# 512-column matmuls in the merge and in both FFNs' first projections of a two-block transformer kernel, with the halves added on two engines

## The chip, the cores and the metric

The kernel runs on one core of one Trainium2 chip. The metric is the device time of one execution in microseconds, as the median of several runs. The core has a matrix engine (PE), which writes only into PSUM, and three engines that matter here besides: DVE (vector), ACT (scalar) and SP, which issues the transfers. Each engine executes its own list of instructions in order and waits on semaphores for the others.

## The reference, cut to what matters

Two transformer blocks over 256 tokens of width 1024, all in 32-bit floats. The first block has an attention branch and a recurrent branch, which are merged under two gates and projected; then comes a gated FFN of hidden width 2816. The second block has other mixers and a convolutional FFN.

```python
ya = jnp.einsum('bse,ed->bsd', y_attn, w_branch_attn[layer])
yb = jnp.einsum('bse,ed->bsd', y_hgrn, w_branch_hgrn[layer])
merged = jax.nn.sigmoid(gate_a) * ya + jax.nn.sigmoid(gate_b) * yb
h = h + jnp.einsum('bsd,de->bse', merged, w_out[layer])
u = rmsnorm(h, norm_ffn_g[layer])
z = (jax.nn.silu(jnp.einsum('bsd,df->bsf', u, w_ffn_gate[layer]))
     * jnp.einsum('bsd,df->bsf', u, w_ffn_up[layer]))
h = h + jnp.einsum('bsf,fd->bsd', z, w_ffn_down[layer])
...
def conv_ffn(h, w_up, conv_w, w_down):
    u = causal_dwconv(h @ w_up, conv_w)
    g, val = jnp.split(u, 2, axis=-1)
    return (jax.nn.silu(g) * val) @ w_down
```

## The kernel before, in words

Activations lie transposed: 128 features on the partitions, 256 tokens along the row, and a 1024-wide activation is 8 such tiles (index `k`). A product in full precision is made of three products in a reduced format: each activation is kept as a high part and a low part, side by side in one tile ([high 256 | low 256]), and each weight tile is split on the chip into `wh` (high) and `wl` (low). `wload` does this for each weight block of 128 x 1024: SP fetches it into `raw` (5 buffers), ACT makes `wh = raw` rounded, and DVE makes `wl = raw - wh` (5 buffers each).

A `gemm` makes one output tile of 128 features x 256 tokens in PSUM, over 8 values of `k` (22 in the FFNs' down projections). For each `k`, `mm3` issues either three 256-column matmuls, which add into the same 256 columns (wh with high, wh with low, wl with high: below "narrow"), or, when it is given a PSUM bank of 512 columns, two matmuls ("wide"): wh with [high | low] into all 512 columns, and wl with high into the upper 256. A wide gemm leaves two halves in PSUM that have to be added to each other.

```python
if ps.n == 2 * S:
    calls = [(ps, a, both, first, last), (ps[:, 1, :], b, hi, False, False)]
    pr.group(calls[::-1] if last else calls)
else:
    pr.group([(ps, a, hi, first, False), (ps, a, lo, False, False), (ps, b, hi, False, last)])
```

Before the change only the down projections use the wide form (7 of their 8 gemms in each FFN); there both halves are added to the residual by two DVE instructions. All else is narrow.

In the order of the program: the first block's mixers (to about 182 us); the merge (gates `wi[T_GA+f]`, `wi[T_GB+f]`, branch projections `wba`, `wbh`, output projection `wo`, 8 gemms each); FFN 1 (`wg`, `wu`: 22 gemms each, of which the first 4 run on activations that aren't normalised yet, then `wd`); the second block's mixers; FFN 2 (`wup`: 44 gemms, the first 4 likewise early, two of them per hidden tile `f`, then 3-tap convolution on DVE, then `wd2`). Between FFN 1's gemms DVE also makes the conditioning vector of the second block: `ada`, 48 products of a fetched 128 x 1024 block (`raw<-in_wada`) with a row held on the chip.

The instruction lists are not written by hand: `record` states the operations, and a list scheduler (`schedule`) orders them on each engine by keys (the PE time at which they are recorded, with offsets for chains and a lead for weights), by modelled durations and by free buffers. An operation made by `either` may go to ACT or DVE: it goes to the second engine only if the first is late, and in the first part of the program only if its key lies `altp1` behind the current time. PSUM has 8 banks, and a bank is handed out per gemm or per two narrow gemms.

Of the kernel before, what the change touches and what calls it, by code (L numbers as in the profile page):

```python
# [10 lines left out]
F32 = mybir.dt.float32  # L11
# [33 lines left out]
for _n, _w in ROW:  # L45
# [7 lines left out]


OPT = dict(
    split=213.902, altp1=0.203, altw1=145.239, o_n3=-12.83, s_n3=0.086, o_f=-0.19, s_f=0.011, lead=9.18,
    tp=2.16, la=42.517, hold=3.107, ahead=1.8, law=0.52, altp=2.588, altw=971.26, ada=0, o_h=11.785, s_h=0.932,
    o_a1=-5.477, s_a1=0.401, o_s=-9.529, s_s=0.517, o_so=-12.055, s_so=0.458, o_a2=1.603, s_a2=0.292,
    o_r=-7.576, s_r=0.015, o_n1=7.29, s_n1=0.166, o_n2=-14.801, s_n2=0.119, o_n4=-10.886, s_n4=0.057,
# [444 lines left out]
def record(pr, d):  # L504
# [13 lines left out]
    def bank2():  # L518
        return bank([P, 2, S])
# [85 lines left out]
    def gemm(ps, src, hl, nk=KD):  # L605
        for k0 in range(0, nk, 8):
            n = min(8, nk - k0)
            w = wload(src[:, k0:k0 + n, :], n * P)
            for i in range(n):
                mm3(ps, w, i, hl, k0 + i, k0 + i == 0, k0 + i == nk - 1)  # L610

    def gemm_multi(ws, pss, hl, parts):
        order = [k for p in parts for k in p]
        for part in parts:
            for j in range(len(pss)):
                for k in part:
                    mm3(pss[j], ws[j], k, hl, k, k == order[0], k == order[-1])
# [414 lines left out]
    hA = hl_of(yA)  # L1032
    ma = Q_all.rearrange("p a b s -> p (a b) s")
    for f in range(8):
        b = bank2()
        gemm(b[:, 0, :], wi[T_GA + f], hl)
        ada(1, OPT["ada"])
        gemm(b[:, 1, :], d["wba"][f], hA)
        sg = pr.tile([P, S], F32, "un", "sga", 3)
        act(sg, b[:, 0, :], AF.Sigmoid, bias=V("b_in", T_GA + f))  # L1040
        tt(ma[:, f, :], b[:, 1, :], sg, ALU.mult)
    yH = pair("yh", "yh")
    for p in range(4):
        f2 = slice(2 * p, 2 * p + 2)
# [3 lines left out]
    mg = pair("ya", "mg")  # L1048
    hH, hM = hl_of(yH), hl_of(mg)
    for f in range(8):  # L1050
        b = bank2()
        gemm(b[:, 0, :], wi[T_GB + f], hl)
        ada(1, OPT["ada"])
        gemm(b[:, 1, :], d["wbh"][f], hH)
        m = pr.tile([P, S], F32, "un", "sgb", 3)
        act(m, b[:, 0, :], AF.Sigmoid, bias=V("b_in", T_GB + f))
        tt(m, b[:, 1, :], m, ALU.mult)
        tt(m, m, ma[:, f, :], ALU.add)
        split(mg[0][:, f, :], mg[1][:, f, :], m)

# [2 lines left out]
    gffn = lambda f: V("norm_ffn_g", f)  # L1063
    for f in range(KD):
        b = bank2()
        gemm(b[:, 0, :], d["wo"][f], hM)
        tt(h[:, f, :], b[:, 0, :], h[:, f, :], ALU.add)
        scaled(xg, h, gffn, f)
        st2.add(h[:, f, :])

# [18 lines left out]
    for p in range(NFF // 2):  # L1089
        if p == 0:  # L1090
            sg = sg0
            for j in range(2):
                tt(sg[:, j, :], sg[:, j, :], r, ALU.mult)
                tt(sg[:, j, :], gb[2 + j][:, 0, :], sg[:, j, :], ALU.mult)
        else:
            b = bank2()
            for j in range(2):
                gemm(b[:, j, :], d["wg"][2 * p + j], hl)
            ada(1, OPT["ada"])
            sg = t2([P, 2, S], "sg")  # L1100
            act(sg, b, AF.Silu)
            b2 = bank2()
            for j in range(2):
                gemm(b2[:, j, :], d["wu"][2 * p + j], hl)
            ada(1, OPT["ada"])
            tt(sg, b2, sg, ALU.mult)
        t, o = divmod(2 * p, 8)
        split(z[t][0][:, o:o + 2, :], z[t][1][:, o:o + 2, :], sg)
    tt(g1e, V("norm_final_g", 0, 8), V("norm_final_g", 0, 8), ALU.mult)
# [256 lines left out]
    for f in range(NFF):  # L1366
        t = t2([P, 2, S], "sg")
        if 2 * f < NG:
            src = [fb[2 * f], fb[2 * f + 1]]
        else:  # L1370
            b = bank2()
            gemm(b[:, 0, :], wup[f], hl)
            gemm(b[:, 1, :], wup[NFF + f], hl)
            src = [b[:, 0, :], b[:, 1, :]]
        for j in range(2):
            g = f + j * NFF
            either(t[:, j, :], src[j], V("fw2", g))
# [149 lines left out]
```

## Time and profile before

| | us |
|---|---|
| median of 3 runs | 767.82 (767.16 to 768.51) |
| the profiled execution, its own time | 766.82 |
| its span, first to last instruction | 765.0 |
| PE busy in the span | 754.7 (99%) |
| DVE busy | 606.1 (79%) |
| ACT busy | 501.6 (66%) |
| granted clock of the matrix engine, mean | 0.998 |

The profiled execution's time is 1.0 us below the median of the runs, and 1.8 us of it lie outside the span. PE's busy time is modelled from pipelined instructions: its length in one row is longer than the distance to the next one's start. So distances between starts tell PE's pace, not the lengths of its rows. The same holds in part on DVE and ACT, whose instructions overlap their successors by some 0.08 us.

### The profile page before, as it was taken

The numbers are of one execution on the slowest core, as the hardware profiler recorded it, in microseconds if no ns is written. First come the engines' busy times: TensorE is split into PE (matmuls) and PEld (weight loads), VectorE is DVE, ScalarE is ACT, GpSimd is POOL, SyncE is SP. The second block draws the span as 40 slices with busy tenths as digits, with TensorE's granted clock in tenths as the row PEclk, the third lists the DMA queues.
The fourth block names the chain that finished last, engine by engine and source line by source line (L and its number), as shares of the span: only waits on it lengthen the run. The fifth ranks groups of instructions, "written<-read, shape, count | busy, mean of one in ns | idle before, by whom it ended". The sixth has DMA issues, their size and how long they took to land.

```text
span 765.0 us, 15411 instructions
## 1 busy us (share of the span) xinstructions
PE 754.7 (99%) x6058; PEld 733.5 (96%) x6058; DVE 606.1 (79%) x1117; ACT 501.6 (66%) x915; POOL 2.2 (0%) x13
## 2 busy tenths in 40 slices
PE   8999999999999999999999999999999999999995
PEld 7999999999999999999998899999999999999885
DVE  6798797877687789877768988988699987887652
ACT  6679999987444666444444457859878766666541
POOL 1000000000000000000000000000000000000000
PEclk9999999999999999999999999999999999999999
DMA  8953444478887558988778985483454775666621
GB/s 296 305 185 117 166 140 138 140 252 287 295 273 242 181 177 279 317 284 280 279 256 260 320 287 193 141 274 114 138 196 136 208 223 180 189 179 179 185 92 55
DMA packets 47512, 161.34 MB, mean 211 GB/s; under 512 B 5568, under 2 KB 7760, under 8 KB 47312
## 3 DMA queue, kind: packets, MB, share of 16 engines
q1 hardware_dynamic: 47152, 160.10, 63.8%
q8 instruction: 47, 0.77, 0.4%
q10 hardware_dynamic: 288, 0.26, 0.1%
q14 instruction: 25, 0.20, 0.1%
HBM read 159.03 MB, written 1.06 MB: 209 GB/s over the span
## 4 chain that ended last, share of the span: by engine, by line
PE 98%; DMA 1%; DVE 0%; SPq 0%; ACT 0%; DVEq 0%; issue 0%
PE ps L307 91%; PE ps L320 3%; PE ps L297 2%; PE ps L327 2%; DMA raw<-in_wv_dram 1%; SPq L334 0%; DVE ot L269 0%; DVE wl L269 0%; ACT wh L229 0%; ACT r L229 0%; DVEq L1522 0%; DVE ot L275 0%; DVE x L275 0%; ACT sql L229 0%
## 5 line engine op out<-in xcount | busy, mean ns | idle before, releaser
L229 ACT ACTIVATE wh<-raw 128x1024 fp32r<-128x1024 f32 (+3 forms) x253 | 258.2, 1028 | 188.5 <-PE ps L307 114.5
L269 DVE TENSOR_TENSOR wl<-raw,wh 128x1024 fp32r<-128x1024 f32 (+3 forms) x255 | 299.0, 1182 | 75.5 <-ACT wh L229 74.4
L307 PE MATMUL ps<-uf,wh 128*128 128x256 f32 x1280 | 226.6, 280 | 0.0
L307 PEld LDWEIGHTS ps<-uf,wh 128*128 128x128 f32 x1280 | 196.9, 189 | 0.0
L307 PE MATMUL ps<-u,wh 128*128 128x256 f32 x976 | 183.2, 287 | 0.0
L307 PE MATMUL ps<-uf,wl 128*128 128x256 f32 x640 | 180.2, 282 | 0.0
L307 PEld LDWEIGHTS ps<-u,wh 128*128 128x128 f32 x976 | 149.4, 189 | 0.8 <-issue 0.4
L307 PE MATMUL ps<-u,wl 128*128 128x256 f32 x488 | 136.9, 281 | 0.0
L307 PE MATMUL ps<-z,wh 128*128 128x512 f32 (+1 forms) x396 | 122.5, 369 | 0.0
L307 PEld LDWEIGHTS ps<-uf,wl 128*128 128x128 f32 x640 | 120.5, 188 | 0.0
L307 PE MATMUL ps<-z,wl 128*128 128x256 f32 x352 | 96.4, 280 | 0.0
L307 PEld LDWEIGHTS ps<-u,wl 128*128 128x128 f32 x488 | 91.9, 188 | 0.0
L275 DVE SCALAR_TENSOR_TENSOR raw<-raw,crow 128x1024 f32<-128x1024 f32 x48 | 58.5, 1222 | 32.1 <-DMA raw<-in_wada_dram 31.2
L307 PEld LDWEIGHTS ps<-z,wh 128*128 128x128 f32 x396 | 70.5, 188 | 12.4
L307 PEld LDWEIGHTS ps<-z,wl 128*128 128x128 f32 x352 | 66.3, 188 | 1.1
L307 PE MATMUL ps<-xg,wh 128*128 128x256 f32 (+1 forms) x256 | 46.5, 284 | 0.0
L307 PEld LDWEIGHTS ps<-xg,wh 128*128 128x128 f32 x256 | 39.6, 189 | 0.2
L229 ACT ACTIVATE ax<-ax,ast 128x256 f32<-128x256 f32 (+1 forms) x82 | 35.2, 447 | 3.9 <-DVE ast L729 3.9
L307 PE MATMUL ps<-xg,wl 128*128 128x256 f32 (+1 forms) x128 | 36.0, 281 | 0.0
L275 DVE SCALAR_TENSOR_TENSOR sg<-ps,vec_t,sg 128x255 f32<-128x255 f32 (+1 forms) x80 | 32.9, 473 | 0.3 <-ACT sg L229 0.3
L307 PE MATMUL ps<-wh,xg 128*128 128x384 f32 x96 | 25.1, 341 | 0.7 <-ACT wh L229 0.7
L307 PEld LDWEIGHTS ps<-xg,wl 128*128 128x128 f32 x128 | 24.4, 190 | 0.0
(259 smaller groups left out, 1024.5 us busy)
## 6 DMA issues: line engine op xcount, KB each, us to landing
raw<-in_wi_dram SPq DMA_DIRECT2D x49, 512.0 KB, 4.6
raw<-in_wada_dram SPq DMA_DIRECT2D x48, 512.0 KB, 4.6
raw<-in_wup_dram SPq DMA_DIRECT2D x44, 512.0 KB, 3.6
raw<-in_wd_dram SPq DMA_DIRECT2D x32, 512.0 KB, 4.2
raw<-in_wg_dram SPq DMA_DIRECT2D x22, 512.0 KB, 4.4
raw<-in_wu_dram SPq DMA_DIRECT2D x22, 512.0 KB, 4.6
raw<-in_w_dram SPq DMA_DIRECT2D x20, 512.0 KB, 4.2
raw<-in_wo_dram SPq DMA_DIRECT2D x16, 512.0 KB, 4.1
```

Source lines behind the costliest of these rows:

```text
L229: self.nc.scalar.activation(out.real(), in_.real(), func, **kw)
L269: f = lambda: self.nc.vector.tensor_tensor(out=out.real(), in0=in0.real(), in1=in1.real(), op=op)
L275: self.nc.vector.scalar_tensor_tensor(out=out.real(), in0=in0.real(), scalar=_real(scalar), in1=in1.real(), op0=op0, op1=op1, **kw)
L297: f = lambda: self.nc.tensor.matmul(out.real(), lhsT.real(), rhs.real(), start=start, stop=stop)
L307: self.nc.tensor.matmul(out.real(), a.real(), b.real(), start=start, stop=stop)
L320: self.nc.tensor.matmul(out.real(), a.real(), b.real(), start=start, stop=stop)
L327: f = lambda: self.nc.tensor.transpose(out.real(), in_.real(), ident.real())
```

## The change

110 gemms are switched from three matmuls per `k` to two: both gates and the attention branch's projection in the merge (24), six of the eight of `wo`, all 40 of FFN 1's `wg` and `wu` that follow the first four, and all 40 of FFN 2's `wup` that follow the first four. Their halves are added by two instructions: ACT copies the upper 256 columns from PSUM to SBUF, DVE adds the lower 256 columns to the copy (`gemm2`); for `wo`, DVE adds both halves to the residual. Each of these gemms now has a PSUM bank of its own. The gate functions read SBUF afterwards. `altp1` goes from 0.203 to 0.576.

```diff
-    split=213.902, altp1=0.203, altw1=145.239, o_n3=-12.83, s_n3=0.086, o_f=-0.19, s_f=0.011, lead=9.18,
+    split=213.902, altp1=0.576, altw1=145.239, o_n3=-12.83, s_n3=0.086, o_f=-0.19, s_f=0.011, lead=9.18,
...
+    def gemm2(out, src, hl, nk=KD):
+
+        b = bank2()
+        gemm(b, src, hl, nk)
+        act(out, b[:, 1, :], AF.Copy)
+        tt(out, b[:, 0, :], out, ALU.add)
...
     for f in range(8):
-        b = bank2()
-        gemm(b[:, 0, :], wi[T_GA + f], hl)
+        sg = pr.tile([P, S], F32, "un", "sga", 3)
+        gemm2(sg, wi[T_GA + f], hl)
+        act(sg, sg, AF.Sigmoid, bias=V("b_in", T_GA + f))
         ada(1, OPT["ada"])
-        gemm(b[:, 1, :], d["wba"][f], hA)
-        sg = pr.tile([P, S], F32, "un", "sga", 3)
-        act(sg, b[:, 0, :], AF.Sigmoid, bias=V("b_in", T_GA + f))
-        tt(ma[:, f, :], b[:, 1, :], sg, ALU.mult)
+        gemm2(ma[:, f, :], d["wba"][f], hA)
+        tt(ma[:, f, :], ma[:, f, :], sg, ALU.mult)
...
     for f in range(KD):
         b = bank2()
-        gemm(b[:, 0, :], d["wo"][f], hM)
-        tt(h[:, f, :], b[:, 0, :], h[:, f, :], ALU.add)
+        wide = f < KD - 2
+        gemm(b if wide else b[:, 0, :], d["wo"][f], hM)
+        for e in range(1 + wide):
+            tt(h[:, f, :], b[:, e, :], h[:, f, :], ALU.add)
...
-            b = bank2()
-            for j in range(2):
-                gemm(b[:, j, :], d["wg"][2 * p + j], hl)
-            ada(1, OPT["ada"])
-            sg = t2([P, 2, S], "sg")
-            act(sg, b, AF.Silu)
-            b2 = bank2()
-            for j in range(2):
-                gemm(b2[:, j, :], d["wu"][2 * p + j], hl)
-            ada(1, OPT["ada"])
-            tt(sg, b2, sg, ALU.mult)
+            sg, su = t2([P, 2, S], "sg"), t2([P, 2, S], "su")
+            for x, w in ((sg, "wg"), (su, "wu")):
+                for j in range(2):
+                    b = bank2()
+                    gemm(b, d[w][2 * p + j], hl)
+                    act(x[:, j, :], b[:, 1, :], AF.Copy)
+                    tt(x[:, j, :], b[:, 0, :], x[:, j, :], ALU.add)
+                ada(1, OPT["ada"])
+                if x is sg:
+                    act(sg, sg, AF.Silu)
+            tt(sg, su, sg, ALU.mult)
...
-            b = bank2()
-            gemm(b[:, 0, :], wup[f], hl)
-            gemm(b[:, 1, :], wup[NFF + f], hl)
-            src = [b[:, 0, :], b[:, 1, :]]
+            src = t2([P, 2, S], "sx")
+            src = [src[:, 0, :], src[:, 1, :]]
+            for j in range(2):
+                gemm2(src[j], wup[f + j * NFF], hl)
```

On PE, in the last gemms of FFN 1's up projections, a `k` was this before (names: `ps` the output, `uf1` the activation, `wh`/`wl` the weight; the number is the tile's):

```order
L307 MATMUL ps_4791<-uf1_3693,wl_4707 128x256
L307 MATMUL ps_4791<-uf1_3693,wh_4696 128x256 x2
L307 MATMUL ps_4791<-uf1_3693,wl_4707 128x256
L307 MATMUL ps_4791<-uf1_3693,wh_4696 128x256 x2
L307 MATMUL ps_4791<-uf1_3693,wl_4707 128x256
```

Now it is two instructions, in the same place:

```order
L307 MATMUL ps_4629<-uf1_3514,wh_4517 128x512
L307 MATMUL ps_4629<-uf1_3514,wl_4538 128x256
L307 MATMUL ps_4629<-uf1_3514,wh_4517 128x512
L307 MATMUL ps_4629<-uf1_3514,wl_4538 128x256
L307 MATMUL ps_4629<-uf1_3514,wh_4517 128x512
```

The order of gemms and of weights on PE is the same there; only the instructions of each are fewer.

On DVE, at the end of FFN 1's up projections, the list before was as follows (`raw,mod<-raw,crow` is an `ada`, `sg<-ps,sg` the product of gate and up projection, `z` its low part for the down projection, `xg3` a small vector):

```order
L269 TENSOR_TENSOR wl_5107<-raw_5018,wh_5096 128x1024
L275 SCALAR_TENSOR_TENSOR raw_5067,mod_2185<-raw_5067,crow_1653 128x1024
L269 TENSOR_TENSOR sg_5072<-ps_5058,sg_5072 128x512
L269 TENSOR_TENSOR xg3_5127<-mod_2185,xg3_5127 128x8x2
L269 TENSOR_TENSOR wl_5143<-raw_5040,wh_5129 128x1024
L269 TENSOR_TENSOR z2_4880<-sg_5072,z2_4880 128x2x256
```

And the list of the change (`su` is the up projection, whose halves are added before the product):

```order
L275 SCALAR_TENSOR_TENSOR raw_4625,mod_2185<-raw_4625,crow_1656 128x1024
L269 TENSOR_TENSOR sg_4665<-ps_4655,sg_4665 128x256
L269 TENSOR_TENSOR wl_4708<-raw_4590,wh_4686 128x768
L269 TENSOR_TENSOR su_4716<-ps_4683,su_4716 128x256
L269 TENSOR_TENSOR wl_4731<-raw_4650,wh_4720 128x1024
L269 TENSOR_TENSOR xg3_4744<-mod_2185,xg3_4744 128x8x2
L275 SCALAR_TENSOR_TENSOR raw_4706,mod_2185<-raw_4706,crow_1656 128x1024
L269 TENSOR_TENSOR su_4716<-ps_4713,su_4716 128x256
L269 TENSOR_TENSOR wl_4764<-raw_4669,wh_4750 128x1024
L269 TENSOR_TENSOR sg_4665<-su_4716,sg_4665 128x512
L269 TENSOR_TENSOR wl_4781<-raw_4691,wh_4772 128x768
L269 TENSOR_TENSOR z2_4560<-sg_4665,z2_4560 128x2x256
```

Between the last `ada` and the last `z` there were a product, the small vector and one weight; now there are an addition, two weights and the product, and the small vector has moved ahead of the `ada`.

On DVE in the middle of FFN 2's up projections, one hidden tile `f` (two gemms) was this before (`sg<-ps` are the convolution's taps on the two halves, `sg<-sg` the product, `z` the low part):

```order
L275 SCALAR_TENSOR_TENSOR sg_8630<-ps_8539,vec_t_67,sg_8630 128x255 x2
L275 SCALAR_TENSOR_TENSOR sg_8630<-ps_8539,vec_t_67,sg_8630 128x254 x2
L269 TENSOR_TENSOR wl_8667<-raw_8498,wh_8652 128x1024
L269 TENSOR_TENSOR sg_8630<-sg_8630 128x256
L269 TENSOR_TENSOR wl_8700<-raw_8537,wh_8688 128x1024
L269 TENSOR_TENSOR z22_8623<-sg_8630,z22_8623 128x256
```

In the change it is this (`sx` is the sum of a gemm's halves):

```order
L269 TENSOR_TENSOR z20_7187<-sg_7463,z20_7187 128x256
L269 TENSOR_TENSOR sx_7470<-ps_7465,sx_7470 128x256
L275 SCALAR_TENSOR_TENSOR sg_7526<-sx_7470,vec_t_67,sg_7526 128x255
L269 TENSOR_TENSOR wl_7556<-raw_7427,wh_7500 128x1024
L275 SCALAR_TENSOR_TENSOR sg_7526<-sx_7470,vec_t_67,sg_7526 128x254
L275 SCALAR_TENSOR_TENSOR sg_7526<-sx_7470,vec_t_67,sg_7526 128x255
L269 TENSOR_TENSOR sx_7536<-ps_7497,sx_7536 128x256
L275 SCALAR_TENSOR_TENSOR sg_7526<-sx_7470,vec_t_67,sg_7526 128x254
L269 TENSOR_TENSOR wl_7587<-raw_7451,wh_7540 128x1024
L269 TENSOR_TENSOR sg_7526<-sg_7526 128x256
L269 TENSOR_TENSOR sx_7536<-ps_7528,sx_7536 128x256
```

Per `f` two additions have come in, the taps read SBUF, and the instructions of two hidden tiles are interleaved more finely.

## Rows read from the trace of the kernel before

**Rows 1.** The page's part 1: busy us of each engine, share, instructions.

```profile
PE 754.7 (99%) x6058; PEld 733.5 (96%) x6058; DVE 606.1 (79%) x1117; ACT 501.6 (66%) x915; POOL 2.2 (0%) x13
```

**Rows 2.** What PE waited for: us in total, times, longest us.

```profile
PE ps L307 <- ACT wh L229: 0.7, 1, 0.7
PE ps L307 <- DVE wl L269: 0.5, 1, 0.5
```

**Rows 3.** Stretches: length, busy us (records) of PE, PEld, DVE, ACT, POOL; clock, DMA.

```profile
45.00:182.00 137.00, 137.00 (x1203) 133.56 (x1202) 112.36 (x251) 129.19 (x305) 0.00 (x0) 1.00 0.51 168
182.00:285.61 103.61, 103.61 (x880) 103.56 (x879) 81.05 (x131) 56.33 (x84) 0.00 (x0) 1.00 0.75 244
285.61:398.89 113.28, 113.28 (x963) 113.28 (x961) 87.58 (x110) 55.77 (x66) 0.00 (x0) 1.00 0.82 277
398.89:452.90 54.01, 54.01 (x311) 47.20 (x310) 46.14 (x75) 25.56 (x35) 0.00 (x0) 1.00 0.87 295
...
581.06:694.31 113.25, 113.25 (x963) 113.25 (x961) 98.46 (x178) 76.23 (x133) 0.00 (x0) 1.00 0.63 193
694.31:748.14 53.83, 53.83 (x310) 47.16 (x309) 32.07 (x44) 28.53 (x39) 0.00 (x0) 1.00 0.48 142
748.14:755.90 7.76, 7.76 (x68) 7.76 (x66) 1.39 (x3) 0.93 (x2) 0.00 (x0) 1.00 0.00 0
```

**Rows 4.** Timeline of PE (start us, us): FFN 1's first and last wide matmul.

```profile
398.89 0.40 PE L307 MATMUL ps<-z,wh 128*128 128x512 f32 x1
...
452.66 0.63 PE L307 MATMUL ps<-z,wh 128*128 128x512 f32 x3
```

**Rows 5.** DVE by form, 592 to 612 us: busy, mean ns of one, idle before.

```profile
L269 DVE TENSOR_TENSOR wl<-raw,wh 128x1024 fp32r<-128x1024 f32 x10 | 12.1, 1215 | 0.0
L275 DVE SCALAR_TENSOR_TENSOR sg<-ps,vec_t,sg 128x255 f32<-128x255 f32 x8 | 3.5, 473 | 0.0
L275 DVE SCALAR_TENSOR_TENSOR sg<-ps,vec_t,sg 128x254 f32<-128x254 f32 x8 | 3.4, 471 | 0.0
L269 DVE TENSOR_TENSOR z<-sg,z 128x256 fp32r<-128x256 f32 x6 | 2.4, 416 | 0.0
L269 DVE TENSOR_TENSOR sg<-sg 128x256 f32<-128x256 f32 x4 | 1.7, 417 | 0.0
```

**Rows 6.** Timeline of DVE in FFN 2's up projections.

```profile
586.32 1.21 DVE L269 TENSOR_TENSOR wl<-raw,wh 128x1024 fp32r<-128x1024 f32 x1
...
594.72 1.22 DVE L269 TENSOR_TENSOR wl<-raw,wh 128x1024 fp32r<-128x1024 f32 x1
...
602.16 1.65 DVE L275 SCALAR_TENSOR_TENSOR sg<-ps,vec_t,sg 128x255 f32<-128x255 f32 x4
...
606.66 1.64 DVE L275 SCALAR_TENSOR_TENSOR sg<-ps,vec_t,sg 128x255 f32<-128x255 f32 x4
```

**Rows 7.** Timeline of DVE: two 256-column instructions reading PSUM, and their successor.

```profile
289.19 0.74 DVE L269 TENSOR_TENSOR sg<-ps,r 128x256 f32<-128x256 f32 x2
289.86 2.35 DVE L269 TENSOR_TENSOR wl<-raw,wh 128x1024 fp32r<-128x1024 f32 x2
```

**Rows 8.** ACT's copies of 256 columns from PSUM: ns min/median/max, first and last start.

```profile
L229 ACT ACTIVATE ya<-ps x4: 387/398/402, 70.8 to 149.0; 128x256 fp32r<-128x256 f32 x4
```

**Rows 9.** Timelines of SP and of DVE at the end of FFN 1's up projections.

```profile
396.16 1.76 SPq L334 DMA_DIRECT2D raw<-in_wada_dram  x2
...
402.16 1.23 DVE L275 SCALAR_TENSOR_TENSOR raw<-raw,crow 128x1024 f32<-128x1024 f32 x1 [3.65 <-DMA raw<-in_wada_dram]
403.31 0.69 DVE L269 TENSOR_TENSOR sg<-ps,sg 128x512 f32<-128x512 f32 x1
...
405.13 0.69 DVE L269 TENSOR_TENSOR z<-sg,z 128x512 fp32r<-128x512 f32 x1
```

**Rows 10.** Timeline of DVE: the last `z` of FFN 2.

```profile
699.33 0.42 DVE L269 TENSOR_TENSOR z<-sg,z 128x256 fp32r<-128x256 f32 x1
```

**Rows 11.** Who waited for whom, longest in total: us, times, longest us.

```profile
ACT wh L229 <- PE ps L307: 114.5, 97, 2.1
```

More of the change, by code (lines that the diff above doesn't have):

```diff
@@ L1050, in record @@
     for f in range(8):
+        m = pr.tile([P, S], F32, "un", "sgb", 3)
+        gemm2(m, wi[T_GB + f], hl)
+        act(m, m, AF.Sigmoid, bias=V("b_in", T_GB + f))
+        ada(1, OPT["ada"])
         b = bank2()
-        gemm(b[:, 0, :], wi[T_GB + f], hl)
-        ada(1, OPT["ada"])
[L1054 to L1057, printed above, removed]
+        gemm(b[:, 0, :], d["wbh"][f], hH)
+        tt(m, b[:, 0, :], m, ALU.mult)
         tt(m, m, ma[:, f, :], ALU.add)
@@ L1095, in record @@
         else:
-            b = bank2()
-            for j in range(2):
-                gemm(b[:, j, :], d["wg"][2 * p + j], hl)
-            ada(1, OPT["ada"])
-            sg = t2([P, 2, S], "sg")
-            act(sg, b, AF.Silu)
-            b2 = bank2()
-            for j in range(2):
-                gemm(b2[:, j, :], d["wu"][2 * p + j], hl)
-            ada(1, OPT["ada"])
-            tt(sg, b2, sg, ALU.mult)
+            sg, su = t2([P, 2, S], "sg"), t2([P, 2, S], "su")
[5 more added lines that the diff above has]
+                    tt(x[:, j, :], b[:, 0, :], x[:, j, :], ALU.add)
+                ada(1, OPT["ada"])
+                if x is sg:
+                    act(sg, sg, AF.Silu)
+            tt(sg, su, sg, ALU.mult)
         t, o = divmod(2 * p, 8)
```

## The prediction

> **What bounds the kernel now.** I read the page's first part, then what PE waited for, then a table by stage. PE is busy for 754.7 of the 765.0 us [rows 1], and after the start-up its recorded waits for the two engines that prepare weights are 0.7 and 0.5 us, once each [rows 2]. In every stretch from 45 to 748 us PE's busy time equals the stretch's length at granted clock 1.00 [rows 3]. So the time is the sum of PE's distances from start to start, and a change counts in two ways only: it makes these distances shorter, or it makes PE wait.
>
> The distances are read from stretches with known content. FFN 1's up projections after the first four gemms are 40 gemms x 8 `k` = 320 narrow triples, from 285.61 to 398.89: 113.28 / 320 = 354.0 ns a triple; FFN 2's are 320 triples from 581.06 to 694.31: 353.9 ns [rows 3]. The down projections hold 7 x 22 = 154 wide pairs. In FFN 1 they start at 398.89 where the row of the first 512-column matmul stands, and the last one starts at 452.66 [rows 4] and is followed by narrow ones at 452.90: 54.01 / 154 = 350.7 ns a pair. In FFN 2 it is 53.83 / 154 = 349.5 ns [rows 3]. The eighth gemm there is narrow again, 22 triples from 748.14 to 755.90: 352.7 ns [rows 3].
>
> The same columns pass in both forms (3 x 256 = 512 + 256), so a pair is cheaper by one instruction's fixed part and by no more: 354.0 less the mean of 350.7 and 349.5 is 3.9 ns. Its bounds are 352.7 - 349.5 = 3.2 ns (the same loop, quiet engines) and 353.9 - 349.5 = 4.4 ns.
>
> **The change: what it saves.** It switches 24 + 6 + 40 + 40 = 110 gemms, each with 8 `k`: 880 instructions fewer on PE. At 3.9 ns that is **-3.4 us**, between -2.8 and -3.9.
>
> The Trainium skill, page "TensorE: Matmul & The Clock Gate", section "Wait — 56ns, not 53.3ns?", gives a fixed cost of about 2.5 ns per matmul on the array at its full clock; by that the saving would be an estimated 2.2 us. The rows of this kernel show 3.2 to 4.4 ns for one matmul less, with its weight load, and I take the rows.
>
> **The change: what it adds.** Each of the 104 gemms with `gemm2` or its like adds one ACT copy of 256 columns, 0.40 us [rows 8], and one DVE addition; six gemms of `wo` add one DVE addition alone. A DVE instruction of this size with an operand in PSUM costs its successor (289.86 - 289.19) / 2 = 0.335 us [rows 7]; its shown length, 0.41, is the upper bound. PE hides this work as long as weights and outputs arrive in time. What is left to each engine, by stage:
> Merge (182 to 285.61): DVE 81.05 + 30 x 0.335 = 91.1 of 103 us. FFN 1: DVE 87.58 + 40 x 0.335 = 101.0 of 112, ACT 55.77 + 16.0 = 71.8. FFN 2: ACT 76.23 + 16.0 = 92.2 of 112, and DVE 98.46 + 13.4 = 111.9 of 112 [rows 3]. The last one is the critical place, since DVE would have no slack left at all over the stretch.
>
> So FFN 2 is taken apart. From 592 to 612 us DVE had no idle time [rows 5]: it was working off what the normalisation before had left. In that state it needed 606.66 - 602.16 = 4.50 us per hidden tile `f` [rows 6], nine instructions (two `wl`, four taps, the product, `z`'s low part), while PE needed 16 x 0.354 = 5.66. With two additions it is 4.50 + 0.67 = 5.17 us, against 16 x 0.350 = 5.60 on PE. DVE keeps a margin of 0.43 us per `f`; it is full because it stays behind its backlog for nearly the whole stretch, not because it is slower than PE. What counts is whether a `wl` is late. Gemm number n (from 0) of the 40 starts at 581.06 + 2.83 n. The order of the weights puts the `wl` at 586.32 to gemm 4 and the one at 594.72 to gemm 6, which starts at 598.05 and has it by 595.94: 2.1 us early [rows 6]. In the order of the change, from the same end of gemm 4's `wl` (587.53, or 6.5 us after the start), I add the distances of what stands ahead of each weight (tap 0.395, addition, product and `z` 0.335 each, `wl` 1.14) up to gemm 12, with 2.80 us per gemm: the smallest lead is about 2.5 us, at gemm 7, and from there it grows by the margin. So no wait there: **0**. The upper bound is rival 1.
>
> In the merge and in FFN 1 the covers are wider: ACT's `wh` waited 114.5 us in total for PE to give weight buffers back [rows 11], so preparation is ahead of PE and is held by the five buffers, not by the engines.
>
> Two joins remain. At the end of FFN 1's up projections the last `z` is needed at `k` = 20 of the first down gemm, 398.89 + 20 x 0.3507 = 405.90. DVE stood waiting for an `ada` transfer until 402.16 (it was issued at 396.16, 6.0 us before), then did the product and ended `z` at 405.13 + 0.69 = 405.82 [rows 9], 0.08 us ahead. In the change there stand between that `ada` and the end of `z` an addition (0.335) and a weight of 768 columns (0.87) more, and the small vector (0.09) less: 1.1 us. If the transfer came at the same distance from the join, PE would wait 1.0 us. The `ada` fetch is issued when DVE gives a `raw` buffer back, which by the new order falls some 0.7 us earlier against the join, so I take a wait of **+0.3 us**, between 0 and 1.0. At the end of FFN 2 the last `z` ended at 699.75 [rows 10], 5.4 us after the join at 694.31, and `k` = 21 is reached at 7.3 us. The new chain has a copy, an addition and the wait of a weight for its buffer more, some 1.3 us together: it ends at 6.7, so 0, at most 0.5.
>
> `altp1` moves a few of the small operations between ACT and DVE in the first 214 us; ACT is busy there for 129.19 of 137 us and DVE for 112.36, and PE never waits [rows 3]. The order of PE's gemms stays, and the cover is the same as now: 0, within 0.5 either way. SP issues the same transfers in the same order.
>
> Sum: -3.4 + 0.3 = -3.1 us. The profiled execution (766.82) would take 763.7; it lies 1.0 below the median of the runs, so the forecast is 767.82 - 3.1 = **764.7 us**. A change under 0.2% (1.5 us) can't be told from none.
>
> **Rivals.**
> 1. *DVE paces FFN 2* (slower). Place: the 20 hidden tiles from 592 us. The margin is 0.43 us per `f`, and it hangs on DVE's instructions overlapping as they did: shown lengths of the nine add to 2 x 1.215 + 2 x 0.473 + 2 x 0.471 + 0.416 + 0.417 = 5.15 us [rows 5] and took 4.50. With two additions of 0.41 the lengths add to 5.97. If none of them overlapped (the new order has taps that need the addition just ahead, by way of ACT), DVE would need 0.37 us more than PE per `f`, 7.4 us over 20, less the lead of 2.5: +4.9, so 769.6. It decides against the change from some 5.9 us per `f`. Against it: the old order had dependent taps too, and DVE lost nothing to them in 20 us. Chance 0.12.
> 2. *The joins eat the gain* (no change that can be told). The `ada` transfer comes as late as now: 1.0 us at the end of FFN 1, 0.5 at the end of FFN 2, with the saving at its lower bound of 2.8: -1.3, so 766.5. For it: 0.08 us of slack now. Against it: the earlier release of the buffer. Chance 0.15.
> 3. *A pair is not cheaper in a gemm of 8 `k`* (the change doesn't do what it says). Wide pairs stand only in gemms of 22 `k` so far, and it could be the longer gemm that is cheaper. Then +0.3 is left: 768.1. Against it: the weights there come in blocks of 8, 8 and 6 `k`, so that their semaphores are nearly as many, and the narrow gemm of 22 `k` in the same loop took 352.7, not 349.5. Chance 0.06.
>
> **How the numbers follow.** The forecast has 0.67. Its own range is -4.2 (3.9 saved, no wait, 0.3 from the first part) to -1.8 (2.8 saved, 1.0 waited): 763.6 to 766.0. The range given reaches from 763.4 to 767.8: it takes in rival 2 and leaves out rival 1 and most of rival 3, and little below. Faster by over 0.2%: 0.67 and a share of rival 2, 0.71. Within: the rest of rival 2 and most of rival 3, 0.16. Slower: rival 1 and a little, 0.13.
>
> **What the profile after would show.** The stretches of the 40 up gemms would last 112.0 us each, at 350 ns a pair, with PE busy throughout; 354 would be rival 3. Among PE's waits DVE's `z` at the first down gemm of FFN 1 would stand with some 0.3 us, over 1 us in rival 2. In FFN 2 DVE would be busy for nearly all of the stretch, in steps of some 5.2 us per `f`, without a row "PE <- DVE wl"; in rival 1 that row has several us and the steps are over 5.6. The prediction is wrong if PE waits anywhere for more than 2 us in total, or if the pitch of the pairs rises because DVE and ACT are busier.

## The result, and the profile after

The changed kernel takes **762.15 us** (median of 4 runs, 762.06 to 762.71); the kernel before took 767.49 in the same session (767.08 to 768.51). The ratio is 0.9927, 95% interval 0.9915 to 0.9938: faster by 0.7%. The forecast was 764.7 with a range from 763.4, so the sign was right and the gain too small: -3.1 us forecast, -5.3 measured. The profiled execution went from 766.82 to 762.06, its span from 765.0 to 760.3. One execution of `g2_wh_steps`, further down, took 1238 us at a granted clock of 0.557 and is left out of its median.

The page's part 1 (as [rows 1]) has 880 PE instructions fewer, and DVE and ACT busier by 36.5 and 31.0 us:

```profile
PE 749.5 (99%) x5178; PEld 691.4 (91%) x5178; DVE 642.6 (85%) x1224; ACT 532.6 (70%) x1022; POOL 2.2 (0%) x13
```

What PE waited for (as [rows 2]; us in total, times, longest):

```profile
PE ps L297 <- POOL eps L539: 1.3, 1, 1.3
PE ps L327 <- ACT ax L229: 0.8, 1, 0.8
PE ps L307 <- DVE wl L269: 0.6, 1, 0.6
PE ps L307 <- ACT wh L229: 0.5, 1, 0.5
```

The `eps`, `wl` and `wh` waits lie in the first 60 us, as before. None stands at the end of an FFN's up projections. One is new: `ax`, 0.8 us, in the second block's mixers.

The stretches (as [rows 3]): merge, `wo` with the first four gemms, FFN 1 up, its down projection, FFN 2 up, its down projection wide and narrow:

```profile
161.82:250.16 88.34, 88.34 (x578) 80.46 (x577) 76.45 (x122) 56.46 (x102) 0.00 (x0) 1.00 0.84 280
250.16:284.45 34.29, 34.29 (x244) 32.09 (x243) 30.13 (x61) 22.73 (x40) 0.00 (x0) 1.00 0.52 170
284.45:395.50 111.05, 111.05 (x643) 97.54 (x641) 100.61 (x150) 67.25 (x103) 0.00 (x0) 1.00 0.89 291
395.50:449.20 53.70, 53.70 (x309) 47.06 (x308) 47.17 (x77) 26.42 (x36) 0.00 (x0) 1.00 0.88 296
...
578.68:689.73 111.05, 111.05 (x643) 97.52 (x641) 110.73 (x216) 88.24 (x172) 0.00 (x0) 1.00 0.63 197
689.73:743.00 53.27, 53.27 (x306) 46.74 (x305) 33.32 (x47) 28.34 (x39) 0.00 (x0) 1.00 0.48 144
743.00:751.20 8.20, 8.20 (x70) 8.12 (x70) 1.39 (x3) 0.93 (x2) 0.00 (x0) 1.00 0.00 0
```

The up projections last 111.05 us where they lasted 113.28 and 113.25 [rows 3]: 111.05 / 320 = **347.0 ns a pair**, 7.0 ns under the triple, and below the 350 ns of the pairs that the kernel had before. That is the surprise. The last two rows are cut 0.5 us ahead of the first narrow matmul (743.52 in PE's timeline), so only their sum says something: 61.47 us, and 61.59 before. The down projections about kept their pitch: (743.52 - 689.73) / 154 = 349.3 ns in FFN 2, where it was 349.5. The merge with `wo` went from 89.57 + 34.49 = 124.06 us (the same two stretches before) to 122.63. So the stages give -2.23 - 2.20 - 1.43 = -5.9 us. The rest of the program gave 1.2 back, 1.0 of it between FFN 1's down projection and the second output projection.

DVE at the end of FFN 1's up projections (as [rows 9]), in FFN 2 (as [rows 6]) and at its last `z` (as [rows 10]):

```profile
396.93 1.22 DVE L275 SCALAR_TENSOR_TENSOR raw<-raw,crow 128x1024 f32<-128x1024 f32 x1 [0.81 <-DMA raw<-in_wada_dram]
...
401.02 0.68 DVE L269 TENSOR_TENSOR z<-sg,z 128x512 fp32r<-128x512 f32 x1
...
598.08 0.87 DVE L275 SCALAR_TENSOR_TENSOR sg<-sx,vec_t,sg 128x254 f32<-128x254 f32 x2
...
603.26 0.88 DVE L275 SCALAR_TENSOR_TENSOR sg<-sx,vec_t,sg 128x254 f32<-128x254 f32 x2
...
695.85 0.43 DVE L269 TENSOR_TENSOR z<-sg,z 128x256 fp32r<-128x256 f32 x1 [0.49 <-ACT z L229]
```

FFN 1's last `z` ends at 401.70, 6.2 us after the join (the start of the down projection), and is needed at 395.50 + 20 x 0.35 = 402.5. In FFN 2 DVE takes 603.26 - 598.08 = 5.18 us per hidden tile.

The pitch (the time of one `k` from start to start) is not one number. Within an up projection whole gemms differ, as PE's timeline shows (starts of the wide matmuls at `k` = 1 and 6 of two gemms of FFN 1):

```profile
315.36 0.39 PE L307 MATMUL ps<-uf,wh 128*128 128x512 f32 x1
...
317.06 0.39 PE L307 MATMUL ps<-uf,wh 128*128 128x512 f32 x1
...
323.64 0.39 PE L307 MATMUL ps<-uf,wh 128*128 128x512 f32 x1
...
325.40 0.40 PE L307 MATMUL ps<-uf,wh 128*128 128x512 f32 x1
```

1.70 / 5 = 340 ns in the first, 1.76 / 5 = 352 in the second, and the pattern comes back every fifth gemm: `wh` and `wl` have five buffers each.

### The profile page after: what moved, and what is told of

Its sections match the earlier page's. It is cut to its first block, busy times and chain, and to the rows that moved or that the text cites. A ratio compares the mean times of both kernels' runs of the same rounds, so it can differ in the third digit from the quotient of the medians.

```text
span 760.3 us, 13881 instructions
## 1 busy us (share of the span) xinstructions
PE 749.5 (99%) x5178; PEld 691.4 (91%) x5178; DVE 642.6 (85%) x1224; ACT 532.6 (70%) x1022; POOL 2.2 (0%) x13
## 4 chain that ended last, share of the span: by engine, by line
PE 96%; DMA 2%; ACT 1%; DVE 1%; SPq 0%; issue 0%; DVEq 0%; ACTq 0%
PE ps L307 90%; PE ps L320 3%; PE ps L327 2%; PE ps L297 2%; DMA raw<-in_wv_dram 1%; DMA adr<-arow 0%; DMA abc<-adr 0%; SPq L334 0%; ACT wh L229 0%; DVE ot L269 0%; DVE mc L275 0%; DVE wl L269 0%; ACT r L229 0%; ACT ax L229 0%; ACT mc L229 0%
## 5 line engine op out<-in xcount | busy, mean ns | idle before, releaser
L307 PE MATMUL ps<-uf,wh 128*128 128x512 f32 x640 | 216.7, 393 | 0.0
L307 PE MATMUL ps<-u,wh 128*128 128x256 f32 (+1 forms) x848 | 183.0, 305 | 0.0
L307 PE MATMUL ps<-uf,wl 128*128 128x256 f32 x640 | 165.8, 279 | 0.0
L307 PEld LDWEIGHTS ps<-u,wh 128*128 128x128 f32 x848 | 134.3, 189 | 4.6 <-issue 0.4
L307 PE MATMUL ps<-u,wl 128*128 128x256 f32 x488 | 134.3, 280 | 0.0
L307 PEld LDWEIGHTS ps<-uf,wh 128*128 128x128 f32 x640 | 114.7, 188 | 20.2
L275 DVE SCALAR_TENSOR_TENSOR sg<-sx,vec_t,sg 128x255 f32<-128x255 f32 x80 | 37.1, 480 | 0.2
L229 ACT ACTIVATE sg<-sx,vec_t 128x256 f32<-128x256 f32 x40 | 20.1, 503 | 6.4 <-DVE sx L269 6.2
```

Of the source, the lines that this page charges most:

```text
L229: self.nc.scalar.activation(out.real(), in_.real(), func, **kw)
L275: self.nc.vector.scalar_tensor_tensor(out=out.real(), in0=in0.real(), scalar=_real(scalar), in1=in1.real(), op0=op0, op1=op1, **kw)
L307: self.nc.tensor.matmul(out.real(), a.real(), b.real(), start=start, stop=stop)
```

## The experiments

In the expectations TensorE, VectorE and ScalarE are PE, DVE and ACT. Lengths by stage in us, from PE's first starts on each operand in the timelines ("merge": from the first matmul on `ya` to FFN 1's fifth gemm; "between": FFN 1's down projection to FFN 2's up projection; "down 2": to the last step). Medians are of the timed runs; the kernel before ran again beside each group of kernels, with medians from 767.49 to 767.93:

```
kernel        median   merge  FFN1 up  between  FFN2 up  down 2
before        767.49  124.06   113.28   182.17   113.25   61.47
changed       762.15  122.63   111.05   183.18   111.05   61.43
e1_swap       762.95  122.63   111.04   183.44   112.16   61.20
e2_altp1      762.24  122.63   111.04   183.15   111.04   61.43
e3_merge      764.29  124.06   111.04   183.97   111.04   61.43
e5_pad        762.58  122.64   111.04   183.85   111.04   61.43
e8_ffn2       765.66  124.05   113.29   184.36   111.04   61.43
e4_dve        770.03  122.64   111.04   184.35   115.38   64.15
e6_place      757.00  121.61   109.92   181.95   109.87   60.42
e7_place_bad  764.09  122.19   112.80   182.18   112.79   61.74
f1_before_bad 765.77  123.68   113.06   183.05   113.07   61.74
f2_all_narrow 767.16  123.67   113.07   183.53   113.06   62.07
f3_before_even 763.75 123.87   113.06   182.39   113.06   60.20
f4_before_bad32 766.31 123.67  113.07   182.44   113.06   61.74
g1_wl_steps   760.02  122.19   110.77   183.15   110.76   61.03
g2_wh_steps   762.98  122.92   111.66   183.49   111.63   60.99
g3_more_wide  757.21  121.32   109.92   183.61   109.86   60.49
```

**Place or kind of gemm: two buffers exchanged.**

```diff
-    u = pair("u", "uf2")
+    u = pair("m", "uf2")
-    z = ztiles("z2", ("m", "yh", "ya"))
+    z = ztiles("z2", ("u", "yh", "ya"))
-    ot = big("u", "ot")
+    ot = big("m", "ot")
```

> The changed kernel, with two buffers of the second FFN exchanged: its input stands where the first of its three z tiles stood (m) and that z tile where the input stood (u). The order of the instructions is the same on TensorE and VectorE. Theory A, the pitch of a wide pair hangs on the place of the moving tile (u 346 ns, yh 348, m and ya 350 in the trace of the changed kernel): the 320 pairs of the second FFN's up projection go from 346 to 350.5 ns, the stage from 111.05 to about 112.5 us, and the down projection's first 8 k steps from 350.7 to 346 (64 steps, -0.3 us): about +1.1 us. Theory B, the pitch hangs on the kind of gemm (8 steps or 22, what the other engines do beside it): both stages as before, within 0.1 us, 0.0 in all.

Measured: 762.95 us. The stretches of both up projections and of FFN 2's wide down gemms (but for their last 0.6 us):

```profile
284.40:395.44 111.04, 111.04 (x642) 97.48 (x641) 100.79 (x150) 67.26 (x103) 0.00 (x0) 1.00 0.88 291
578.88:691.04 112.16, 112.16 (x643) 98.21 (x642) 111.14 (x216) 87.72 (x172) 0.00 (x0) 1.00 0.61 195
691.04:744.00 52.96, 52.96 (x306) 46.51 (x305) 33.29 (x47) 28.29 (x39) 0.00 (x0) 1.00 0.50 145
```

FFN 2 up rose by 1.11 us to 350.5 ns a pair, FFN 1 up stayed, FFN 2 down fell by 0.23. The pitch goes with the buffer and not with the kind of gemm: theory B (the kind of gemm sets it) falls.

**One part at a time.** The planner's number back; the merge narrow again (two lines of it shown, the gates with theirs); and, from there, FFN 1 narrow (its gemms' lines shown) and the number back too, so that FFN 2 alone is wide.

```diff
-altp1=0.576
+altp1=0.203
```

> The changed kernel with the planner's number altp1 as it was before the change (0.203). My forecast was that the number is worth 0 within 0.5 us. If it is what lengthens the mixers of the second block by 1.2 us in the changed kernel, this kernel is 1.2 us faster there; if it was chosen well for the new loads, it is slower by 0.3 to 1 us, in the first block or in the merge; if it does nothing, within 0.2 us.

```diff
-        gemm2(ma[:, f, :], d["wba"][f], hA)
+        gemm(b[:, 1, :], d["wba"][f], hA)
-        wide = f < KD - 2
+        wide = False
```

> The changed kernel with the merge of the branches narrow again (three 256-column matmuls for each k in the gates, the two branch projections and the output projection): 240 more TensorE instructions. At my forecast's 3.9 ns for each the merge was worth 0.9 us, at the 7 ns that the FFNs showed 1.7 us, and by the merge's stage in the two traces (89.57 to 88.34 and 34.49 to 34.29 us) 1.4 us: this kernel is slower than the changed one by that.

```diff
-                    gemm(b, d[w][2 * p + j], hl)
+                gemm(b[:, j, :], d["wg"][2 * p + j], hl)
+                gemm(b2[:, j, :], d["wu"][2 * p + j], hl)
```

> Of the change only the second FFN's up projection (320 pairs instead of 320 triples), all else as in the kernel before. By the stage in the two traces (113.25 to 111.05 us) it is worth 2.2 us: about 765.4. It is also a second look at the mixers of the second block with everything ahead of them as before: if their 1.0 us more in the changed kernel (83.1 to 84.3 us from the first wide input to the output projection; a PE wait of 0.8 us that is not in the profile of before) comes from what the change does ahead of them, it is gone here; if it is the round trip of the small row through device memory, which takes 1.9 us in the profile of before and 2.2 to 3.4 in the others, it can be here too.

`altp1` is worth nothing (762.24). The merge is worth 122.63 - 124.06 = -1.43 us in its own stage, as 5.9 ns for each of 240 instructions (the run is 2.1 slower in all, 0.8 of it "between"). FFN 2 is worth -2.21 us (stretches of the kernel with FFN 2 alone wide):

```profile
285.53:398.82 113.29, 113.29 (x963) 113.29 (x962) 88.15 (x111) 56.36 (x66) 0.00 (x0) 1.00 0.82 277
583.18:694.22 111.04, 111.04 (x642) 97.45 (x641) 110.72 (x216) 88.24 (x172) 0.00 (x0) 1.00 0.64 197
```

In that kernel all is as before ahead of the mixers, and "between" is longer still (184.36): PE waited 1.0 us for FFN 1's last `z` and 0.4 for `ax`. SP's rows show one thing that differs ahead of the second block's attention, a small row's round trip through device memory, here of the changed kernel and, second, of the kernel before:

```profile
507.31 0.34 SPq L334 DMA_DIRECT2D adr<-arow  x1
...
510.75 1.75 SPq L334 DMA_DIRECT2D abc<-adr  x4
```

```profile
510.84 0.34 SPq L334 DMA_DIRECT2D adr<-arow  x1
...
512.74 1.75 SPq L334 DMA_DIRECT2D abc<-adr  x4
```

The small row's write to device memory took 3.4 us until its readers could be issued, 1.9 before, and in the other kernels profiled up to `e5_pad` 2.2 to 3.3. But it does not account for the stage: it took 3.4 in `e6_place` (below), where "between" is shortest, and 2.1 in `e8_ffn2`, where it is longest. "Between" varies from 181.95 to 184.36 over kernels whether or not FFN 1 is wide, so the 1.0 us given back there can't be put down to the change, and its cause stays open.

**DVE's margin in FFN 2**, rival 1:

```diff
                 gemm2(src[j], wup[f + j * NFF], hl)
+                tt(src[j], src[j], src[j], ALU.max)
```

> The changed kernel with one more VectorE operation for each half-sum in the second FFN's up projection (an elementwise maximum of the sum with itself, 40 in all, which changes no value). It asks how near VectorE is to setting the pace there: it is busy 110.73 of 111.05 us in the trace of the changed kernel. If it is full, 40 more operations of about 0.3 us cost up to 12 us less what the planner moves to ScalarE (busy 88 of 111 us): +3 to +10 us, with TensorE waiting on VectorE. If its busy time is stretched by waits inside its queue and there is room, under 0.5 us.

Measured: 770.03 us, ratio to the kernel before 1.0032 (1.0020 to 1.0045). The stretch, the waits of PE's weight loads in it, one hidden tile on DVE, then PE's waits from 695 us on:

```profile
579.68:695.06 115.38, 114.84 (x642) 95.63 (x641) 114.81 (x238) 88.98 (x167) 0.00 (x0) 1.00 0.56 176
```

```profile
PEld ps L307 <- DVE wl L269: 8.3, 25, 1.0
```

```profile
601.60 0.47 DVE L275 SCALAR_TENSOR_TENSOR sg<-sx,vec_t,sg 128x254 f32<-128x254 f32 x1
...
607.46 0.47 DVE L275 SCALAR_TENSOR_TENSOR sg<-sx,vec_t,sg 128x254 f32<-128x254 f32 x1
```

```profile
PE ps L307 <- DVE wl L269: 1.7, 2, 1.3
```

The stage is 4.3 us longer and the down projection behind it 2.7. `wl` came late 25 times, and DVE took 607.46 - 601.60 = 5.86 us per hidden tile where PE needs 16 x 0.347 = 5.55: DVE set the pace. So the changed kernel has less than one 256-column operation per half-sum of room, and rival 1 was the right danger. The margin per hidden tile, forecast at 0.43 us, is 5.55 - 5.18 = 0.37 in the changed kernel, and the two operations cost 5.86 - 5.18 = 0.68.

**Which place.** First all buffers 704 bytes up, by an unused one ahead of them.

```diff
+        pad.tile([P, 176], F32, tag="pad", name="pad", bufs=1)
```

> The changed kernel with every buffer of SBUF moved up by 704 bytes, nothing else. If the pitch of a wide pair hangs on where a tile begins within a row of 2 KB (now u 1760, yh 1440, m 1056, ya 128), then m takes u's remainder and its pitch (the first 8 k steps of both down projections near 346 ns), and u with remainder 416 loses its own: up projections from 111.05 to about 112.3 us each, some +2 us in all. If it hangs on the region of SBUF, or on the kind of gemm and not on the place, all stages stay within 0.2 us.

No stage of wide pairs moved: the place of a tile within a row of 2 KB does not set the pitch. But the five-gemm pattern says that the weights' buffer counts too. So two placements were made to order: the buffers named in `PADS` come first in SBUF, in this order, each with so many unused f32 columns ahead of it. The order of the instructions is unchanged. The first ("even"), and what the second ("bad") has in its place:

```diff
-RAW = 1040
+RAW, WCOL = 1040, 1088
+PADS = [('wh', 0), ('wl', 16), ('yh', 0), ('m', 0), ('u', 0), ('ya', 32)]
-        wh = pr.tile([P, RAW], F32R, "wh", "wh", NW)
-        wl = pr.tile([P, RAW], F32R, "wl", "wl", NW)
+        wh = pr.tile([P, WCOL], F32R, "wh", "wh", NW)
+        wl = pr.tile([P, WCOL], F32R, "wl", "wl", NW)
```

```diff
+PADS = [('wh', 0), ('wl', 0), ('yh', 48), ('m', 0), ('u', 0), ('ya', 32)]
```

> The changed kernel with the same order of instructions and other addresses in SBUF: the five buffers of wh and the five of wl are 4352 bytes apart instead of 4160 (17 x 256 instead of 65 x 64), and they and the four large activation buffers are put first, so that for every wide pair the weights begin at the same remainder of 256 bytes from the activations: wl 0, wh 192. In the trace of the changed kernel the pairs of the up projections fall into five groups by weight buffer, and the two groups with these remainders run at 340.0 ns a pair in both FFNs (the other three at 347, 348 and 352; in the down projections' buffers 343 to 355). Theory C, the pitch of a wide pair hangs on the place of the weights relative to the activations (the remainder of 256 bytes): all pairs go to 340 ns, up projections 111.05 to about 109.3 us each, down projections by 308 x 10 ns = 3.1 us less, the merge by 1.9 us less, in all some -8.5 us, near 753.7. Theory A, the region of SBUF alone: pairs keep values of 346 to 350 or move to new ones without one value for all buffers; theory B, the kind of gemm: up 111.05 and down as now. The narrow triples, 351 to 357 ns by weight buffer before, were 354 to 355 in these two buffers: no change expected for them.

> As the kernel with equal remainders, but with wl and wh both 64 bytes past the activations (remainder of 256), the group that is slowest in the changed kernel's up projections (352 ns). Theory C: every wide pair at 352 ns: up projections 111.05 to about 113.2 us each, down projections +0.6 us, the merge +1 us, about 767.5 in all, as slow as the kernel before. Theories A and B: no more than 0.5 us from the other placement.

Up projections in the first and in the second placement:

```profile
283.59:393.51 109.92, 109.92 (x642) 96.97 (x641) 100.20 (x150) 67.02 (x103) 0.00 (x0) 1.00 0.87 292
575.46:685.33 109.87, 109.87 (x643) 96.94 (x641) 109.56 (x215) 88.23 (x171) 0.00 (x0) 1.00 0.63 198
```

```profile
283.78:396.58 112.80, 112.80 (x643) 98.23 (x641) 101.21 (x150) 67.23 (x103) 0.00 (x0) 1.00 0.86 287
578.76:691.55 112.79, 112.79 (x642) 98.20 (x641) 111.40 (x216) 88.03 (x172) 0.00 (x0) 1.00 0.62 194
```

757.00 and 764.09 us. All five buffers went to 341 to 342 and to 352 to 353 ns, with the same instructions in the same order, so the place of the weights relative to the activations moves the wide pitch; the region of SBUF, nearly the same in both, does not (theory A falls). The even placement gained 5.2 us over the changed kernel where 8.5 was expected: its up projections are shorter by 1.1 and 1.2 us (1.75 expected), the merge by 1.0 (1.9) and FFN 2's down projection by 1.0 (1.5). In the bad one the up and down projections met the expectation to 0.4 us. The merge did not: it came out 0.4 us below the changed kernel where 1 us above was expected, since its narrow gemms took 340 ns, as narrow gemms did elsewhere, and the kernel was 3.4 us faster than expected. The even one is the fastest kernel here (`g3_more_wide`, below, is within 0.2 us): ratio to the kernel before 0.9865 (0.9852 to 0.9877).

**The same placements for the kernel before**: bad; bad and all narrow; even; bad and 32 bytes up.

> The kernel before the change (all first projections narrow) with the placement of the second placement run: wl and wh both 64 bytes past the activations (remainder of 256). In that run the wide pairs took 352 to 353 ns, and the narrow triples that were left (w2, the output projection, xg2) took 340.0 ns where they take 354 in the kernel before. Theory D, the place sets the pitch of narrow and wide apart, and the change's gain belongs to the placement: the 1490 or so narrow triples go from 354 to 340, -20.9 us, the 308 wide pairs of the down projections from 350 to 352, +0.8: about 747.5 us, and at this placement the change is a loss of some 16 us (764.1 with it). Rival: the 340 ns belongs to those gemms and not to the placement; FFN stages stay at 113.3 us, about 763 to 767.

```diff
-        wide = f < KD - 1
+        wide = False
-        gemm(b, d["wd2"][f], hz2, NFF)
-        for e in range(2):
+        gemm(b[:, 0, :], d["wd2"][f], hz2, NFF)
+        for e in range(1):
```

> The same, with the down projections of both FFNs narrow as well (14 gemms of 22 steps: 308 more TensorE instructions, 14 fewer additions on VectorE). Theory D: 308 x 12 to 13 ns less than the run beside it, -3.8 us, about 743.7. Against it: the price of one more instruction for each k step, 3.9 ns in my forecast and 7 ns in the changed kernel, would make it 1.2 to 2.2 us slower.

> The kernel before the change with the placement of the first placement run (wl 0, wh 192 past the activations), in which wide pairs took 341 to 343 ns and the narrow triples left 353.5. Theory D: up projections as before, 113.1 to 113.3 us each, down projections 308 x 8 ns = 2.5 us less: about 764.8, so that at this placement the change is worth some -7.8 us (757.0 with it).

```diff
-PADS = [('wh', 0), ('wl', 0), ('yh', 48), ('m', 0), ('u', 0), ('ya', 32)]
+PADS = [('wh', 8), ('wl', 0), ('yh', 48), ('m', 0), ('u', 0), ('ya', 32)]
```

> As the first of these four, with every buffer another 32 bytes up, so that none begins at a multiple of 64 as none of the large ones but one does in the kernel before; the remainders between weights and activations stay 64 and 64. In the kernel before, the one pair of weight buffers with these remainders (none at a multiple of 64) took 353.3 ns a triple, not 340. If the multiple of 64 is what is wanted beside the remainder: triples at 353 to 354, 766 to 768. If only the remainders count: 747.5 as the first.

Theory D (the place sets the narrow pitch as well, and the gain belongs to the placement) falls. In the FFNs the triple takes 113.06 / 320 = 353.3 ns in each of the four (shown: the first), and the kernel with all gemms narrow is 1.4 us slower than the one beside it, not 3.8 faster.

```profile
284.42:397.48 113.06, 113.06 (x962) 113.06 (x961) 87.90 (x110) 55.92 (x66) 0.00 (x0) 1.00 0.82 278
580.53:693.60 113.07, 113.07 (x962) 113.07 (x961) 98.54 (x178) 76.36 (x133) 0.00 (x0) 1.00 0.63 194
```

Narrow triples have a second level all the same, 340 ns, and the place alone does not set it. In the bad placement the eighth gemm of FFN 1's down projection is narrow in both of the first two kernels and, by the program's allocation, uses the same buffers. Behind seven wide gemms it took 340 ns a triple, behind seven narrow ones 353 (starts six `k` apart, first and second kernel; 2.04 / 6 and 2.12 / 6):

```profile
455.16 0.39 PE L309 MATMUL ps<-z,wh 128*128 128x256 f32 x2
...
457.20 0.39 PE L309 MATMUL ps<-z,wh 128*128 128x256 f32 x2
```

```profile
454.99 0.40 PE L309 MATMUL ps<-z,wh 128*128 128x256 f32 x2
...
457.11 0.40 PE L309 MATMUL ps<-z,wh 128*128 128x256 f32 x2
```

The narrow gemms of the merge took 340 in `e7_place_bad`, where wide ones run ahead of them, and 353 in `f1_before_bad`. The second output projection took 353 in the first of the four runs and 340 in the fourth, which has the same order and the same distances. So neither the place nor the order alone sets the level: what ran ahead counts, its waits perhaps, and how is open.

The change is worth 762.15 - 767.49 = -5.3 us where the buffers stood, -6.8 in the even placement (757.00 against 763.75) and -1.7 in the bad one (764.09 against 765.77). By stage the even one is worth more, 2.3 + 3.1 + 3.2 = 8.6 us: the profiled execution of `f3_before_even` lay 1.6 us above its median. Of the 1.7 in the bad one little belongs to the pairs: the up projections gave 0.3 us each, and the 1.5 of the merge is about what its 112 narrow triples (second branch projection, two of `wo`, FFN 1's first four) save at 340 instead of 353.3 ns (1.49). The down projection in FFN 2, wide in the kernel before as well, took 60.20 us in the even placement against 61.47 where the buffers stood. In the bad one it took 61.74 with seven wide gemms and 62.07 all narrow, and 0.28 of these 0.33 us is the eighth gemm's level.

One of the twelve executions of `f1_before_bad` took 760.71 us, 5.1 below the median. It has no trace. One up projection at 340 ns would save 320 x 13.3 ns = 4.3 us (an estimate); that this happened there is not shown.

**Which of the two remainders.** From the even placement, one of the two back to 4160 bytes from buffer to buffer; the activations' pad was set so that the other stays at its distance.

```diff
-        wl = pr.tile([P, WCOL], F32R, "wl", "wl", NW)
+        wl = pr.tile([P, RAW], F32R, "wl", "wl", NW)
```

> The changed kernel in the placement with equal remainders, but the five wl buffers 4160 bytes apart again: wh begins 192 past the activations (remainder of 256) for all five, wl 0, 64, 128, 192 and 0. If the remainder of wl alone sets the pitch of a wide pair: 341 ns in the two buffers with 0, 350 to 354 at 64, 347 at 128, 348 at 192 (the values of the changed kernel's up projections at these remainders of wl), mean 345.5, and up projections of 111.0 us. If wh alone does: all five at 341, 109.9 us. If both together do: the two with 0 at 341, the others anywhere from 340 to 354.

```diff
-        wh = pr.tile([P, WCOL], F32R, "wh", "wh", NW)
+        wh = pr.tile([P, RAW], F32R, "wh", "wh", NW)
```

> The counterpart: wl 0 past the activations for all five buffers, wh 192, 0, 64, 128 and 192. If wl alone sets the pitch: all at 341, up projections 109.9 us, as the placement with equal remainders (757.0 in all). If wh alone: 341 at 192, 347 at 0, 352 at 64, 348 at 128, 341 at 192, 111.0 us.

Mean pitches in ns by weight buffer, from the starts of wide and narrow matmuls in PE's timelines of the up projections (inner `k` steps, 40 of each and FFN; in `e1_swap` FFN 2), with wl's and wh's distance from the activations (remainder of 256):

```
changed       0/192: 340 340   128/0: 347  192/128: 348   64/64: 352
e1_swap (m)   192/128: 353 348  64/192: 347   0/0: 354   128/64: 353
e6_place      0/192: 341 to 342, all five
e7_place_bad  64/64: 352 to 353, all five
g1_wl_steps   0/192: 341 340   64/192: 347   128/192: 350  192/192: 349
g2_wh_steps   0/192: 349 345   0/0: 348   0/64: 345   0/128: 352
```

With wh held, wl moves the pitch by 10 ns; with wl held, wh moves it by 7. Neither alone sets it, and the remainder of 256 is not the whole rule: 0/192 gave means of 345 and 349 in the last kernel, and 192/128 gave 348 and 353 in the exchanged one. Nor is the place the whole rule. The 345 is a mean of two levels: two gemms of `g2_wh_steps` five apart, so with the same `wh`, `wl` and activation, took (309.52 - 307.82) / 5 = 340 and (323.48 - 321.73) / 5 = 350 ns (starts at `k` = 1 and 6):

```profile
307.82 0.39 PE L309 MATMUL ps<-uf,wh 128*128 128x512 f32 x1
...
309.52 0.39 PE L309 MATMUL ps<-uf,wh 128*128 128x512 f32 x1
...
321.73 0.40 PE L309 MATMUL ps<-uf,wh 128*128 128x512 f32 x1
...
323.48 0.40 PE L309 MATMUL ps<-uf,wh 128*128 128x512 f32 x1
```

The PSUM bank is not the difference: by the program's allocation this weight buffer with bank 5 had 340 in FFN 1 and 350 in FFN 2. As with the narrow triples, something seems to be carried over from what ran ahead. The rule stays open.

**More of the same.** In the even placement, gates `T_HG`, `wbh` and the queries also by `gemm2`.

```diff
-            gemm(b[:, j, :], wi[T_HG + 2 * p + j], hl)
+            gemm2(sg[:, j, :], wi[T_HG + 2 * p + j], hl)
-        gemm(b[:, 0, :], d["wbh"][f], hH)
+        gemm2(mb, d["wbh"][f], hH)
-            gemm(qb[:, 0, :], wi[T_AQ + j], hl)
+            gemm2(q, wi[T_AQ + j], hl)
```

> The placement with equal remainders and 24 more wide gemms of 8 steps: the last gates of the first mixer (8), the second branch projection of the merge (8) and the queries of the first attention (8), each with a ScalarE copy and a VectorE addition more. At 341 a pair against 353.5 a triple: 192 x 12.5 ns = -2.4 us, about 754.6, if the additions are hidden there (VectorE is less busy in the mixers than in the FFNs); if they lengthen the chain to the first attention or the merge, -1 us to +1 us.

757.21 us, no gain. The merge fell by 0.3 us, the first mixers ended 0.5 us earlier, and "between" was 1.7 us longer (PE waited 1.1 for `ax` and 1.0 for `z`), a stretch that this edit does not touch. Expected were 754.6 us.

## Why the forecast was too small

- **The bound, and what counts**: right. PE's busy share is 99%, and the stages account for the difference.
- **The saving**: this step failed: "a pair is cheaper by one instruction's fixed part and by no more", 3.9 ns between 3.2 and 4.4, 880 x 3.9 = 3.4 us. It measured 6.9 to 7.0 ns in the FFNs and 5.9 in the merge, 5.9 us. The price came from the down projections' pairs, as if a pair had one pitch. Pairs take 340 to 354 ns by where `wl`, `wh` and the activations lie, and, it seems, by what ran ahead; FFN 1's and FFN 2's input stood in a buffer where two of the five weight buffers give 340, and the `z` tiles did not. The exchange of buffers shows it with the order of the instructions unchanged. That the step erred towards a larger gain was luck: in the bad placement a pair in the FFNs is only 353.3 - 352.5 = 0.8 ns cheaper than the triple, in the even one 353.3 - 343.4 = 9.9 ns (whole stages). The Trainium skill ("TensorE: Matmul & The Clock Gate", section "Wait — 56ns, not 53.3ns?") states a fixed cost of about 2.5 ns per matmul. The traces here agree with no one fixed cost: one matmul and weight load less was worth 0.8 to 10 ns a step.
- **The additions hidden**: right. DVE was forecast busy 101.0 and 111.9 us in the FFNs and was 100.61 and 110.73; 5.17 us per hidden tile, measured 5.18; no `wl` late. (The prediction speaks of nine DVE instructions per hidden tile; its list and its sums have eight, and nothing hangs on it.)
- **The joins**: +0.3 forecast, 0 measured. The `ada` transfer cost DVE 0.81 us of waiting instead of 3.65 [rows 9], and `z` came 0.8 us early. Other kernels with the same or the old FFN 1 waited 1.0 there, so the bounds of 0 and 1.0 were fair. FFN 2's last `z` was forecast 6.7 us after the join and ended at 6.55.
- **`altp1`**: 0, and measured 0.1.
- **Rival 3** (a pair is not cheaper in a gemm of 8 `k`) was opposite to the truth: 347.0 ns there against 349.3 in the gemms of 22 `k`. **Rival 2** did not come. **Rival 1** was not reached, and `e4_dve` shows that it is close.
- Two sizes that the prediction did not have: the 1.0 us that "between" took back, whose cause stays open; and the profiled execution of before lay 0.7 us below its median, that of after 0.1, so the medians differ by 0.6 more than the profiles.

## What to carry to other kernels

A pitch read from a trace holds for the buffers that it was read in and for what ran ahead of it: before pricing a matmul form by it, split it by weight buffer and by activation tile, look gemm by gemm and not at means alone, and take the spread as the range. Where PE is the bound, try the buffers' places before more arithmetic: here the better of two placements was worth 5.2 us over the changed kernel, nearly as much as the change, and the other cost 1.9. And where an edit moves work to an engine that is full, price one operation more on the chip, since 40 operations turned -5.3 into +2.5.

## What had not been expected of the hardware

Five buffers that the program treats alike gave pairs of 340, 340, 347, 348 and 352 ns, alike in both FFNs to about 1 ns. The Trainium skill ("SBUF — State Buffer", section "A bandwidth-pool intuition that's wrong (but worth ruling out)") gives TensorE a second, independent read port for weight loads. One would expect from it that the place of the weights does not matter to the moving data; 341 against 352 ns in two placements of the same program show that the place does matter, and no run here shows whether a port is the reason. Narrow triples kept 353 to 354 in the FFNs (means of whole stages) in every placement, and had a second level, 340, elsewhere. Both forms also changed level at one and the same place: the narrow one in the eighth down gemm (340 or 353), the wide one in `g2_wh_steps` (340 or 350). What ran ahead seems to decide there; the rule was not found.
